# A two-layer trunk at its layer boundary: the branch output is turned to tokens in place of the sum, four chunks of weights are split ahead instead of three, and x is read a second time

## The chip, the cores and the metric

The kernel runs on one core of one Trainium2 chip. The metric is the device time of one execution in microseconds. Engines are named as in the profile: PE is TensorE (PEld its weight loads), ACT is ScalarE, DVE is VectorE, POOL is GpSimd, SP is SyncE, which issues nearly all loads.

## The reference

Two layers, each `h <- h + RMSNorm(mixer(RMSNorm(h)))`. The first mixer is differential attention, the second a pooling mixer; the boundary between them is the subject here.

```python
h = concatenate([meta, x], axis=1)                  # 272 tokens x 2048
y = diff_attention_mixer(rms_norm(h, pre_norm_g[0]), ...)   # ends in (o * silu(g)) @ w_out
h = h + rms_norm(y, post_norm_g[0])
proj = rms_norm(h, pre_norm_g[1]) @ w_in            # pooling mixer
u, g = split(proj, 2)                               # each 2048 wide
mixed = einsum(pooled(u) - u, w_group) * scale      # 4 groups, windows 2, 4, 8, 16
y = (mixed * silu(g)) @ w_out
h = h + rms_norm(y, post_norm_g[1])
return h[:, 16:]                                    # without the meta tokens
```

## The kernel before

Activations lie with features on the 128 partitions and tokens (272) along the free axis, 16 k-tiles deep. All products are in float32 made of reduced-precision parts: a chunk of weights (128x2048, 1 MB) is loaded as `raw`, cast by ACT into `hi`, and the rest `lo = raw - hi` is taken by DVE (`split`, lines 97 and 98). `mm3` makes three matmuls of each k-tile: `hi` by `hi`, `hi` by `lo`, `lo` by `hi` (lines 121 to 123). Chunks are numbered in the order of use: 64 to 79 are the output weights of attention (products `py0` to `py15`, one per chunk, 48 matmuls each), 80 to 95 the first products of the pooling mixer, `pu0` on, with the group weights of the mixing (`pm`) in between. `take` splits the chunk in use and the next and loads the one after. `raw` has two buffers, `hi` and `lo` three each, so a split waits until PE has done with the chunk three before it. Eight banks of PSUM go round in turn.

Each engine runs its instructions in one fixed order, which the framework's scheduler makes from the program text; `issue_after` pins an instruction behind another.

At the boundary (from line 541): each `py` is squared by ACT and summed by DVE into `sqy`, the last into `sqz`; ACT copies it into `yg` with the gain of the post-norm. `Norm` makes the means of squares by one-column matmuls for three groups of tokens (16, 128, 128), DVE scales them (`v`), POOL raises to -1/2, and `spread` lays the result along the free axis by three matmuls. Around that, 14 `busy` matmuls of 128 columns write a bank that nobody reads. Then for each k-tile, in nine steps of one or two k-tiles, DVE makes `yg *= pr` and `h1 += yg`, ACT the `hi` part (`hh`) with the gain of the pre-norm, DVE the `lo` part (`hl`), and PE runs the k-tile for `NS = 3` chunks at once:

```python
        for j in range(k, k + n):
            for u in range(NS):
                u_part(u, j)
```

The fourth, `pu3`, follows in quarters, with its chunk split in quarters in between (`hi_u`, `lo_u`). Chunks 84 and 85 are split into `ms`, in the home of the finished attention output. The squares of `h1` are folded by DVE into `sq1`, from which a second norm's scale is made in the middle of `pu5`. After `pu5`, `pu7`, `pu9` and `pu10`, `turn_h` turns eight blocks of `h1` to tokens (PE transposes into PSUM, ACT copies into `ht`): at the end of the program the output by tokens is `ht` plus the second branch. From `pu5` on DVE pools (`pooled`), up to the inputs `zs` of the mixing.

Of the kernel before, what the change touches and what calls it, by code (L numbers as in the profile page):

```python
# [16 lines left out]
P = 128  # L17
D = 2048
# [25 lines left out]
def trunk(ctx: ExitStack, tc: tile.TileContext, first, hT, small, gpost1, rope, w_in, w_out, p_in, p_grp, p_out, out):  # L44
# [112 lines left out]
    class Norm:  # L157
# [3 lines left out]
        def __init__(self, sq, name, r=None, more=None):  # L161
            self.pb = bank(f"rms_{name}")
            v = self.mean(sq, name, EPS)
            if more is not None:
                v = self.mean(more, name + "b", v)
            self.r = r if r is not None else const.tile([P, 3], F32, tag="nr", name=f"r_{name}")
            pool.tensor_tensor(out=self.r, in0=v, in1=mhalf, op=ALU.pow)

        def mean(self, sq, name, plus):
            c = 505 if isinstance(plus, float) else 508  # L170
# [393 lines left out]

# [268 lines left out]
```

## Time and profile before

| | |
|---|---|
| median of 3 runs | 845.69 us (845.52 to 846.54) |
| the profiled execution's own time | 845.79 us |
| its span, first to last instruction | 844.0 us |
| PE, DVE, ACT busy | 832.3, 580.0, 432.0 us |

The profile is of one execution. A matmul's row is longer than the step from one matmul to the next, since they overlap; steps are read from the starts. Matmuls of plain float32 (norm and dummies) have two rows each, transposes one.

### The profile page before, as it was taken

The page shows a single profiled execution, that of the slowest core. Times are in us where ns is not written, and L with a number is a line of the kernel's source. Part 1 is how long each engine was busy: PE and PEld are TensorE (multiplying, and loading weights), DVE is VectorE, ACT ScalarE, POOL GpSimd, SP SyncE. Part 2 cuts the span into 40 slices and gives each one's busy share as a digit, 9 for nine tenths or more (in the row PEclk, how much of TensorE's full clock was granted, in tenths as well). Part 3 has the DMA queues.
Part 4 walks back from the last instruction along what each step waited for, and adds up shares of the span by engine and source line. Part 5 has one row for each costly group of instructions (what it writes and reads, how often), then busy time and mean ns, then how long its engine had stood idle before and what let it go on. Part 6 is the DMA issues. An engine that isn't in the chain of part 4 may idle for free.

```text
span 844.0 us, 14596 instructions
## 1 busy us (share of the span) xinstructions
PE 832.3 (99%) x6140; PEld 803.3 (95%) x6140; DVE 580.0 (69%) x936; ACT 432.0 (51%) x673; POOL 7.3 (1%) x16
## 2 busy tenths in 40 slices
PE   9999999999999999999999999999999999999996
PEld 9999999999999999999999999999999888888896
DVE  6789767686868587887754444787877766685423
ACT  8646546464646466864434444544544445563420
POOL 0100000000000000000000000000000000000000
PEclk9999999999999999999999999999999999999999
DMA  9445344444444444354557455153565455545412
GB/s 352 168 151 204 149 157 164 162 164 151 150 150 151 153 158 163 128 199 152 195 206 279 174 188 211 59 201 141 196 254 184 167 199 200 189 161 206 194 50 100
DMA packets 22242, 147.27 MB, mean 174 GB/s; under 512 B 2592, under 2 KB 3104, under 8 KB 5664
## 3 DMA queue, kind: packets, MB, share of 16 engines
q1 hardware_dynamic: 22032, 146.30, 48.0%
q8 instruction: 48, 0.79, 0.4%
q14 instruction: 18, 0.15, 0.0%
q10 hardware_dynamic: 144, 0.04, 0.0%
HBM read 144.23 MB, written 2.10 MB: 173 GB/s over the span
## 4 chain that ended last, share of the span: by engine, by line
PE 94%; DVE 2%; issue 1%; DMA 1%; ACT 0%; POOL 0%; DVEq 0%; POOLq 0%; ACTq 0%
PE p L121 14%; PE p L122 14%; PE p L123 14%; PE pv L129 7%; PE py L122 4%; PE py L121 4%; PE py L123 4%; PE pv L130 4%; PE pz L725 3%; PE pz L724 3%; PE pz L723 3%; PE pu L122 3%; PE pu L123 3%; PE pu L121 3%; PE pm L129 2%
## 5 line engine op out<-in xcount | busy, mean ns | idle before, releaser
L98 DVE TENSOR_TENSOR lo<-raw,hi 128x2048 fp32r<-128x2048 f32 x121 | 276.9, 2288 | 141.5 <-ACT hi L97 141.2
L97 ACT CAST hi<-raw 128x2048 fp32r<-128x2048 f32 x121 | 231.2, 1910 | 193.0 <-PE p L122 96.0
L121 PE MATMUL p<-xs,hi 128*128 128x272 f32 x928 | 269.6, 290 | 0.0
L122 PE MATMUL p<-xs,hi 128*128 128x272 f32 x928 | 268.5, 289 | 0.0
L123 PE MATMUL p<-xs,lo 128*128 128x272 f32 x928 | 268.0, 289 | 0.0
L121 PEld LDWEIGHTS p<-xs,hi 128*128 128x128 f32 x928 | 174.9, 188 | 0.0
L123 PEld LDWEIGHTS p<-xs,lo 128*128 128x128 f32 x928 | 174.6, 188 | 0.0
L122 PEld LDWEIGHTS p<-xs,hi 128*128 128x128 f32 x928 | 174.5, 188 | 0.0
L129 PE MATMUL pv<-hs,hi 128*128 128x512 f32 x256 | 89.5, 393 | 0.0
L122 PE MATMUL py<-os,hi 128*128 128x272 f32 x256 | 74.3, 290 | 0.0
L123 PE MATMUL py<-os,lo 128*128 128x272 f32 x256 | 73.8, 288 | 0.0
L121 PE MATMUL py<-os,hi 128*128 128x272 f32 x256 | 73.7, 288 | 0.0
L130 PE MATMUL pv<-hs,lo 128*128 128x256 f32 x256 | 71.8, 280 | 0.0
L129 PEld LDWEIGHTS pv<-hs,hi 128*128 128x128 f32 x256 | 48.1, 188 | 10.9
L123 PE MATMUL pu<-hs,lo 128*128 128x264 f32 (+3 forms) x192 | 54.6, 285 | 0.0
L122 PE MATMUL pu<-hs,hi 128*128 128x264 f32 (+3 forms) x192 | 54.5, 285 | 0.0
L121 PE MATMUL pu<-hs,hi 128*128 128x264 f32 (+3 forms) x192 | 54.4, 287 | 0.0
L121 PEld LDWEIGHTS py<-os,hi 128*128 128x128 f32 x256 | 48.3, 189 | 0.0
L123 PEld LDWEIGHTS py<-os,lo 128*128 128x128 f32 x256 | 48.2, 188 | 0.0
L130 PEld LDWEIGHTS pv<-hs,lo 128*128 128x128 f32 x256 | 48.1, 188 | 0.0
L122 PEld LDWEIGHTS py<-os,hi 128*128 128x128 f32 x256 | 48.0, 188 | 0.0
L724 PE MATMUL pz<-lo,zs 128*128 128x512 f32 (+1 forms) x128 | 46.4, 363 | 0.0
(249 smaller groups left out, 1362.5 us busy)
## 6 DMA issues: line engine op xcount, KB each, us to landing
raw<-in_w_in SPq DMA_DIRECT2D x60, 1024.0 KB, 4.8
raw<-in_p_in SPq DMA_DIRECT2D x32, 1024.0 KB, 4.8
raw<-in_w_out SPq DMA_DIRECT2D x16, 1024.0 KB, 4.8
raw<-in_p_out SPq DMA_DIRECT2D x14, 1024.0 KB, 4.8
pk<-in_first SPq DMA_DIRECT2D x6, 784.0 KB, 10.7
raw<-in_p_grp SPq DMA_DIRECT2D x4, 1024.0 KB, 4.8
h<-in_hT SPq DMA_DIRECT2D x4, 544.0 KB, 7.2
rawx<-in_p_out SPq DMA_DIRECT2D x2, 1024.0 KB, 7.1
```

Source lines behind the costliest of these rows:

```text
L97: act.copy(hi[:, s], raw[i][:, s])
L98: rest[i] = dve.tensor_tensor(out=lw[:, s], in0=raw[i][:, s], in1=hi.bitcast(F32)[:, s], op=ALU.subtract)
L121: pe.matmul(o, wh, xh, start=first, stop=False)
L122: pe.matmul(o, wh, xl, start=False, stop=False)
L123: pe.matmul(o, wl, xh, start=False, stop=last)
L129: pe.matmul(ps[:, 0:2 * n], wh, x, start=first, stop=False, skip_group_check=not first)
L130: pe.matmul(ps[:, 0:n], wl, x[:, 0], start=False, stop=last)
L723: pe.matmul(ps, zh[:, k, s], wh[:, c], start=k == 0, stop=False)
L724: pe.matmul(ps, zh[:, k, s], wl[:, c], start=False, stop=False)
L725: pe.matmul(ps, zl[:, k, s], wh[:, c], start=False, stop=k == KT - 1)
```

## The change

The 32 transposes of `h1` and the 14 dummies go. In their place `yg`, the branch output with its gain but before its norm, is turned around the norm: sixteen blocks ahead of the spread, sixteen behind it. The first four banks are copied by ACT and DVE, the others by ACT between its first `hh`. Later in layer 1 DVE makes `ht = ht * rcol + xtok`, `rcol` the norm's scale by tokens and `xtok` the input x, loaded a second time by tokens into the home of `h1`. The first means (of `sqy`) move into `py15`, ahead of its last two k-tiles. Four chunks are split ahead while `py` runs: 80 and 81 into `ms`, now in the home of the attention input, from a `raw` buffer of their own (`rawu`); 82 and 83 into `hi` and `lo`. `NS` is 4, and every k-tile is a step of its own; only the first reads the spread from PSUM, the others its copy `prs`. Chunk 84 is split in two halves behind k-tile 9, chunk 85 as any other.

```diff
+            self.name, self.v = name, None
+            self.mean(sq)
+            if not wait:
+                self.power(r)
+
+        def mean(self, sq):
+        def power(self, r=None):
+            self.r = r if r is not None else const.tile([P, 3], F32, tag="nr", name=f"r_{self.name}")
+            pool.tensor_tensor(out=self.r, in0=self.v, in1=mhalf, op=ALU.pow)
...
-    def proj(ps, n0, n1, rh, rl, mid=None):
+    def proj(ps, n0, n1, rh, rl, mid=None, at=KT // 2):
...
-    NS = 3
+    NS = 4
     IU = cur[0] + KT
+
+    ms = base.tile([P, 2, 2, CW], F32R, tag="xs", name="ms")
+    ht = l1.tile([P, 2, D], F32, tag="ht", name="ht")
+    rcol = const.tile([P, 3], F32, name="rcol")
+    norm = []
-        proj(ps, 0, L, oh, ol)
-        t = sqy if m == 0 else sqz if m == KT - 1 else l1.tile([P, L], F32, tag="tmp", name=f"sqy{m}", bufs=2)
+        proj(ps, 0, L, oh, ol, (lambda: norm.append(Norm(sqy, "post0", wait=True))) if m == KT - 1 else None, KT - 3)
+        if m == KT - 1:
+            split(IU + 3)
+            break
+        t = sqy if m == 0 else l1.tile([P, L], F32, tag="tmp", name=f"sqy{m}", bufs=2)
-        if 0 < m < KT - 1:
+        if m:
...
-        if m >= KT - 5:
-
-            if m == KT - 5:
-                ht = l1.tile([P, 2, CW], F32R, tag="ht", name="w_spare")
-                split(IU, dst=(ht[:, 0, :], ht[:, 1, :]))
-            elif m >= KT - 3:
-                split(IU + m - KT + 3)
-                load(IU + m - KT + 4)
-                load(IU + m - KT + 5)
-
-
-    hs = base.tile([P, 2, KT, L], F32R, tag="xs", name="hs")
+        if m in (5, 8, 11):
+
+            q = (5, 8, 11).index(m)
+            raw[IU + q] = l1.tile([P, CW], F32, tag="rawu", name=f"rawu{q}")
+            nc.sync.dma_start(raw[IU + q], chunks[IU + q])
+        elif m == 13:
+            load(IU + 3)
+        elif m == 14:
+            split(IU + 2)
+        elif m in (7, 10):
+            q = (7, 10).index(m)
+            split(IU + q, dst=(ms[:, 0, q, :], ms[:, 1, q, :]))
+
+
+    norm = norm[0]
+    tb = [bank(f"yt{i}") for i in range(4)]
+
+    def turn_y(g, j0=0, j1=4):
+        q, b = divmod(g, 2)
+        for j in range(j0, j1):
+            i = pe.transpose(tb[g % 4][:, j * P:(j + 1) * P], yg[:, 4 * q + j, TOK[b + 1][0]:TOK[b + 1][1]], ident)
+        if j1 == 4 and g < 4:
+            turned(g, dve.tensor_copy if g in (1, 2) else act.copy)
+        return i
+
+    def turned(g, copy):
+        q, b = divmod(g, 2)
+        copy(ht[:, b, 4 * q * P:(4 * q + 4) * P], tb[g % 4])
+
+    act.square(sqz, ps[:, 0:L])
+    turn_y(0)
+    t = turn_y(1, 0, 2)
+    with tc.issue_after(t.ins):
+        norm.mean(sqz)
+    t = act.activation(yg[:, m, :], ps[:, 0:L], AF.Copy, scale=sp[:, C_POST0 + m:C_POST0 + m + 1])
+    norm.power(rcol)
+    with tc.issue_after(norm.last.ins):
+        turn_y(1, 2, 4)
+        turn_y(2)
+        t = turn_y(3)
+    with tc.issue_after(t.ins):
+        pr = norm.spread()
+        t = norm.last
+    with tc.issue_after(t.ins):
+        for g in range(4, 8):
+            t = turn_y(g)
+
...
+    prs = l1.tile([P, L], F32, name="prs")
...
-    load(i0 + NS + 1)
-    norm = Norm(sqy, "post0", more=sqz)
-    with tc.issue_after(norm.last.ins):
-        busy(5)
-    pr = norm.spread()
-    busy(9)
-    accu = [bank(f"pu{t}") for t in range(NS + 1)]
...
-    halves[i0 + NS] = (wpool.tile([P, CW], F32R, tag="hi", name="hi_u"), wpool.tile([P, CW], F32R, tag="lo", name="lo_u"))
-    k, hhs = 0, []
-    for n in (1, 1, 2, 2, 2, 2, 2, 2, 2):
-
-        ks = slice(k, k + n)
-        dve.tensor_tensor(out=yg[:, ks, :], in0=yg[:, ks, :], in1=pr.unsqueeze(1).broadcast_to([P, n, L]), op=ALU.mult)
-        dve.tensor_tensor(out=h1[:, ks, :], in0=h1[:, ks, :], in1=yg[:, ks, :], op=ALU.add)
-        for j in range(k, k + n):
-            g = sp[:, C_PRE1 + j:C_PRE1 + j + 1]
-            t = act.activation(hh[:, j, :], h1[:, j, :], AF.Copy, scale=g)
-            hhs.append(t)
-            dve.scalar_tensor_tensor(out=hl[:, j, :], in0=h1[:, j, :], scalar=g, in1=hh.bitcast(F32)[:, j, :],
+    hhs, add = [], None
+    for k in range(KT):
+
+        with (tc.issue_after(add.ins) if add else ExitStack()):
+            dve.tensor_tensor(out=yg[:, k, :], in0=yg[:, k, :], in1=prs if k else pr, op=ALU.mult)
+            if k == 0:
+                act.copy(prs, pr)
+            add = dve.tensor_tensor(out=h1[:, k, :], in0=h1[:, k, :], in1=yg[:, k, :], op=ALU.add)
+        g = sp[:, C_PRE1 + k:C_PRE1 + k + 1]
+        with (tc.issue_after(hhs[-1].ins) if hhs else ExitStack()):
+            hhs.append(act.activation(hh[:, k, :], h1[:, k, :], AF.Copy, scale=g))
+        t = dve.scalar_tensor_tensor(out=hl[:, k, :], in0=h1[:, k, :], scalar=g, in1=hh.bitcast(F32)[:, k, :],
-        for j in range(k, k + n):
-            for u in range(NS):
-                u_part(u, j)
-        k += n
-        if k in (4, 6, 8, 10):
-            with tc.issue_after(t.ins):
-                split_part(i0 + NS, slice((k - 4) * 256, (k - 2) * 256))
-        if k in (6, 8, 12, 16):
-            q = (6, 8, 12, 16).index(k)
-            for j in range(4 * q, 4 * q + 4):
-                u_part(NS, j)
-    cur[0] += 1
-
-    ms = base.tile([P, 2, 2, CW], F32R, tag="os", name="ms")
-    mh, ml = ms[:, 0], ms[:, 1]
-    with tc.issue_after(hhs[9].ins):
-        split(cur[0], dst=(mh[:, 0, :], ml[:, 0, :]))
-    load(cur[0] + 1)
+        if k < 4:
+            with tc.issue_after(hhs[-1].ins):
+                turned(4 + k, act.copy)
+        for u in range(NS):
+            u_part(u, k)
+        if k == 9:
+            with tc.issue_after(hhs[-1].ins), tc.issue_after(t.ins):
+                split(cur[0], 2)
...
-        act.square(yf[:, s], hf[:, s])
+        with tc.issue_after(hhs[min(4 * q + 7, KT - 1)].ins):
+            act.square(yf[:, s], hf[:, s])
+    load(cur[0] + 1)
-    split(cur[0] + 1, dst=(mh[:, 1, :], ml[:, 1, :]))
-
-
-    ht = l1.tile([P, 2, D], F32, tag="ht", name="ht")
...
-            if t > NS:
+            if t >= NS:
                 accu.append(bank(f"pu{t}"))
-                proj(accu[t], un0(t), L, hh, hl, (lambda: norm1.append(Norm(sq1, "pre1"))) if t == NS + 2 else None)
-                if t == NS + 2:
+                proj(accu[t], un0(t), L, hh, hl, (lambda: norm1.append(Norm(sq1, "pre1"))) if t == NS + 1 else None)
+                if t == NS + 1:
                     act.copy(r1, norm1[0].spread())
                     for i in range(t):
                         pooled(i, accu[i])
-                if t >= NS + 2:
+                if t >= NS + 1:
                     pooled(t, accu[t])
-            if t in (5, 7, 9, 10):
-                turn_h((5, 7, 9, 10).index(t))
+            if t == 7:
+                xtok = l1.tile([P, 2, D], F32, tag="h1", name="xtok")
+                for b in range(2):
+                    nc.sync.dma_start(xtok[:, b, :], xt[b * P:(b + 1) * P, :])
+            if t in (12, 13):
+
+                b = t - 12
+                with tc.issue_after(rest[cur[0]].ins):
+                    for c in (slice(0, D // 2), slice(D // 2, D)):
+                        dve.scalar_tensor_tensor(out=ht[:, b, c], in0=ht[:, b, c], scalar=rcol[:, b + 1:b + 2],
+                                                 in1=xtok[:, b, c], op0=ALU.mult, op1=ALU.add)
         elif kind == "m":
             mixing(t)
         else:
@@ -744,7 +777,7 @@
                                      op0=ALU.mult, op1=ALU.add)
             nc.sync.dma_start(out[b * P:(b + 1) * P, c], ht[:, b, c])
 
```

PE at the boundary before, from the last k-tile of `py15` to the first of `pu` (`rms_post0` is the norm's bank, `Activation`, `DVE` and `Pool` name engines waited for):

```order
L121 MATMUL py15_5998<-os_536,hi79_5936 128x272
L122 MATMUL py15_5998<-os_536,hi79_5936 128x272
L123 MATMUL py15_5998<-os_536,lo79_5937 128x272
L172 MATMUL rms_post0_6057<-ones_75,sqy_5106 128x1 [waits DVE_49]
L172 MATMUL rms_post0_6057<-ones_75,sqy_5106 128x1 x2
L172 MATMUL rms_post0_6057<-ones_75,sqz_5107 128x1 [waits DVE_49,Activation_49]
L172 MATMUL rms_post0_6057<-ones_75,sqz_5107 128x1 x2
L136 MATMUL busy_6070<-ones_75 128x128 x5
L182 MATMUL rms_post0_6057<-ident_70,r_post0_6068 128x16 [waits Pool_49]
L182 MATMUL rms_post0_6057<-ident_70,r_post0_6068 128x128 x2
L136 MATMUL busy_6079<-ones_75 128x128 x9
L121 MATMUL pu0_6089<-hs_6055,w_spare_5808 128x258 [waits PE_49,Activation_49]
```

PE at the same place now, from the last k-tile of `py15`:

```order
L121 MATMUL py15_6002<-os_536,hi79_5942 128x272
L122 MATMUL py15_6002<-os_536,hi79_5942 128x272
L123 MATMUL py15_6002<-os_536,lo79_5943 128x272
L581 MATMUL yt0_6061<-ident_70,yg_5095 128x128 x4
L581 MATMUL yt1_6062<-ident_70,yg_5095 128x128 x2
L171 MATMUL rms_post0_6045<-ones_75,sqz_5107 128x1 [waits DVE_49,Activation_49]
L171 MATMUL rms_post0_6045<-ones_75,sqz_5107 128x1 x2
L581 MATMUL yt1_6062<-ident_70,yg_5095 128x128 x2
L581 MATMUL yt2_6063<-ident_70,yg_5095 128x128 x4
L581 MATMUL yt3_6064<-ident_70,yg_5095 128x128 x4
L185 MATMUL rms_post0_6045<-ident_70,rcol_5110 128x16 [waits Pool_49]
L185 MATMUL rms_post0_6045<-ident_70,rcol_5110 128x128 x2
```

The dummies are gone, ten blocks stand between the second means and the spread and sixteen behind it, each group of four of these behind the copy of its bank; the first means stand two k-tiles ahead of the rows shown.

DVE from the second `v` on, before:

```order
L177 SCALAR_TENSOR_TENSOR v_post0b_6066<-rms_post0_6057,v_post0_6061 128x3 [waits DVE_49,PE_49]
L589 TENSOR_TENSOR yg_5095<-yg_5095,rms_post0_6057 128x272 [waits PE_49]
L589 TENSOR_TENSOR yg_5095<-yg_5095,rms_post0_6057 128x272
L590 TENSOR_TENSOR h1_5099<-h1_5099,yg_5095 128x272 [waits DVE_49] x2
L589 TENSOR_TENSOR yg_5095<-yg_5095,rms_post0_6057 128x544
L595 SCALAR_TENSOR_TENSOR hs_6055<-h1_5099,sp_67,hs_6055 128x272 [waits Activation_49] x2
L590 TENSOR_TENSOR h1_5099<-h1_5099,yg_5095 128x544 [waits DVE_49]
L589 TENSOR_TENSOR yg_5095<-yg_5095,rms_post0_6057 128x544
```

DVE from the second `v` on, now:

```order
L176 SCALAR_TENSOR_TENSOR v_post0_508_6076<-rms_post0_6045,v_post0_505_6049 128x3 [waits DVE_49,PE_49]
L588 COPY ht_5109<-yt1_6062 128x512 [waits PE_49]
L588 COPY ht_5109<-yt2_6063 128x512 [waits PE_49]
L631 TENSOR_TENSOR yg_5095<-yg_5095,rms_post0_6045 128x272 [waits PE_49]
L634 TENSOR_TENSOR h1_5099<-h1_5099,yg_5095 128x272 [waits DVE_49]
L631 TENSOR_TENSOR yg_5095<-yg_5095,prs_6114 128x272 [waits Activation_49]
L634 TENSOR_TENSOR h1_5099<-h1_5099,yg_5095 128x272 [waits DVE_49]
L638 SCALAR_TENSOR_TENSOR hs_6112<-h1_5099,sp_67,hs_6112 128x272 [waits Activation_49]
L631 TENSOR_TENSOR yg_5095<-yg_5095,prs_6114 128x272
L638 SCALAR_TENSOR_TENSOR hs_6112<-h1_5099,sp_67,hs_6112 128x272 [waits Activation_49]
```

Two copies of turned blocks stand ahead of the first product; products and sums are of one k-tile each, in turn.

DVE at the end of the k-tiles, before:

```order
L98 TENSOR_TENSOR ms_6345<-raw84_6053,ms_6345 128x2048 [waits DMAHW2_49]
L98 TENSOR_TENSOR ms_6345<-raw85_6348,ms_6345 128x2048 [waits DMAHW3_49,Activation_49]
L595 SCALAR_TENSOR_TENSOR hs_6055<-h1_5099,sp_67,hs_6055 128x272 [waits Activation_49] x2
L107 TENSOR_TENSOR yg_5095<-yg_5095 128x2176 [waits Activation_49]
L107 TENSOR_TENSOR yg_5095<-yg_5095 128x1088 [waits DVE_49]
L107 TENSOR_TENSOR yg_5095<-yg_5095 128x544 [waits DVE_49]
L98 TENSOR_TENSOR lo86_6417<-raw86_6365,hi86_6416 128x2048 [waits DMAHW4_49,PE_49,Activation_49]
```

DVE at the end of the k-tiles, now:

```order
L634 TENSOR_TENSOR h1_5099<-h1_5099,yg_5095 128x272 [waits DVE_49]
L638 SCALAR_TENSOR_TENSOR hs_6112<-h1_5099,sp_67,hs_6112 128x272 [waits Activation_49] x2
L107 TENSOR_TENSOR yg_5095<-yg_5095 128x2176 [waits Activation_49]
L107 TENSOR_TENSOR yg_5095<-yg_5095 128x1088 [waits DVE_49]
L107 TENSOR_TENSOR yg_5095<-yg_5095 128x544 [waits DVE_49]
L98 TENSOR_TENSOR lo85_6403<-raw85_6393,hi85_6402 128x2048 [waits DMAHW3_49,PE_49,Activation_49]
L107 TENSOR_TENSOR sq1_6388<-yg_5095 128x272 [waits DVE_49]
L98 TENSOR_TENSOR lo86_6458<-raw86_6406,hi86_6457 128x2048 [waits DMAHW4_49,PE_49,Activation_49]
```

Before, both splits into `ms` stood ahead of the last `hl` and of the three folds; now the split of chunk 85, `pu5`'s, stands behind the folds.

## Rows read from the trace of the kernel before

**Rows 1.** The page: the chain that ended last, share of the span by engine.
```profile
PE 94%; DVE 2%; issue 1%; DMA 1%; ACT 0%; POOL 0%; DVEq 0%; POOLq 0%; ACTq 0%
```

**Rows 2.** Chain of waits, 528 to 560 us: start, length, what.
```profile
528.92 0.40 ACT sqz L546
...
532.75 0.79 DVE yg L589 x2
...
536.33 0.63 DVE yg L589
...
539.71 0.82 DVE hs L595 x2
540.54 0.60 DVE lo_u L213
...
546.61 6.69 DMA raw<-in_p_in
...
555.25 2.29 DVE ms L98
```

**Rows 3.** Timeline of PE, 528 to 575 us: start, length, engine, line, operation.
```profile
528.59 0.29 PE L123 MATMUL py<-os,lo 128*128 128x272 f32 x1
...
529.79 0.80 PE L172 MATMUL rms_post<-ones,sqz 128*128 128x1 f32 x6 [0.34 <-ACT yg L549]
...
531.78 0.93 PE L182 MATMUL rms_post<-ident,r_post 128*128 128x16 f32 x6
...
534.50 0.38 PE L121 MATMUL pu<-hs,w_spare 128*128 128x258 f32 x1
...
554.37 0.28 PE L123 MATMUL pu<-hs,lo 128*128 128x258 f32 x1
555.70 0.39 PE L121 MATMUL pu<-hs,w_spare 128*128 128x258 f32 x1 [1.05 <-ACT hs L593]
...
560.51 0.28 PE L121 MATMUL pu<-hs,ms 128*128 128x260 f32 x1
...
568.63 0.28 PE L123 MATMUL pu<-hs,ms 128*128 128x260 f32 x1
...
569.33 0.36 PE L121 MATMUL pu<-hs,ms 128*128 128x260 f32 x1
...
571.92 0.83 PE L182 MATMUL rms_pre<-ident,r_pre 128*128 128x16 f32 x6
572.59 1.29 PE L631 MATMUL ht<-ident,h 128*128 128x128 f32 x8
573.86 0.39 PE L121 MATMUL pu<-hs,hi 128*128 128x260 f32 x1
```

**Rows 4.** Busy time by stretch, matmuls of `pu` alone: stretch, length, PE, PEld.
```profile
534.50:573.86 39.36, 35.76 (x288) 34.74 (x288) 0.00 (x0) 1.00 0.37 134
```

**Rows 5.** Timeline of PE at a later block of transposes; the tile `ht`.
```profile
585.30 0.28 PE L123 MATMUL pu<-hs,lo 128*128 128x260 f32 x1
...
586.22 0.37 PE L121 MATMUL pu<-hs,hi 128*128 128x264 f32 x1
...
L632 ACT COPY ht<-ht x8: 570/585/597, 573.2 to 612.7; 128x512 f32<-128x512 f32 x8
```

**Rows 6.** Timeline of DVE, 500 to 580 us.
```profile
526.89 0.43 DVE L548 TENSOR_TENSOR sqy<-sqy,sqy 128x272 f32<-128x272 f32 x1
...
558.29 4.50 DVE L107 TENSOR_TENSOR yg<-yg 128x2176 f32<-128x2176 f32 x3
```

**Rows 7.** The tile `py` (first and last start); loads by line, us to landing.
```profile
L121 PE MATMUL py<-os,hi x256: 287/288/289, 431.9 to 528.3; 128*128 128x272 f32 x128
...
gp<-in_gpost SPq DMA_DIRECT2D x1, 1024.0 KB, 10.2
```

**Rows 8.** Timeline of PE at the start of the program.
```profile
6.72 0.42 PE L237 MATMUL pq<-xs,flo 128*128 128x272 f32 x1
6.95 0.32 PE L238 MATMUL pq<-xs,fhi 128*128 128x272 f32 x1
```

More of the change, by code (lines that the diff above doesn't have):

```diff
@@ L43, in trunk @@
 @with_exitstack
-def trunk(ctx: ExitStack, tc: tile.TileContext, first, hT, small, gpost1, rope, w_in, w_out, p_in, p_grp, p_out, out):
+def trunk(ctx: ExitStack, tc: tile.TileContext, first, hT, xt, small, gpost1, rope, w_in, w_out, p_in, p_grp, p_out, out):
     nc = tc.nc
@@ L157, in trunk, with __init__ @@
     class Norm:
-        def __init__(self, sq, name, r=None, more=None):
+        def __init__(self, sq, name, r=None, wait=False):
             self.pb = bank(f"rms_{name}")
[L163 to L170, printed above, removed]
+            self.name, self.v = name, None
[3 more added lines that the diff above has]
+        def mean(self, sq):
+            c = 505 if self.v is None else 508
             for j in range(3):
                 self.last = pe.matmul(self.pb[:, c + j:c + j + 1], sq[:, WIN[j]:WIN[j] + P], ones[:, 0:1], start=True, stop=True)
-            v = const.tile([P, 3], F32, tag="nv", name=f"v_{name}", bufs=2)
-            if isinstance(plus, float):
-                self.vi = dve.tensor_scalar(out=v, in0=self.pb[:, c:c + 3], scalar1=1.0 / D, scalar2=plus, op0=ALU.mult, op1=ALU.add)
-            else:
-                dve.scalar_tensor_tensor(out=v, in0=self.pb[:, c:c + 3], scalar=1.0 / D, in1=plus, op0=ALU.mult, op1=ALU.add)
-            return v
+            v = const.tile([P, 3], F32, tag="nv", name=f"v_{self.name}_{c}", bufs=2)
+            if self.v is None:
+                self.vi = dve.tensor_scalar(out=v, in0=self.pb[:, c:c + 3], scalar1=1.0 / D, scalar2=EPS, op0=ALU.mult, op1=ALU.add)
+            else:
+                dve.scalar_tensor_tensor(out=v, in0=self.pb[:, c:c + 3], scalar=1.0 / D, in1=self.v, op0=ALU.mult, op1=ALU.add)
+            self.v = v
+        def power(self, r=None):
+            self.r = r if r is not None else const.tile([P, 3], F32, tag="nr", name=f"r_{self.name}")
+            pool.tensor_tensor(out=self.r, in0=self.v, in1=mhalf, op=ALU.pow)
         def spread(self):
             for j, (a, b) in enumerate(TOK):
-                pe.matmul(self.pb[:, a:b], self.r[:, j:j + 1].broadcast_to([P, P]), ident[:, 0:b - a], start=True, stop=True)
+                self.last = pe.matmul(self.pb[:, a:b], self.r[:, j:j + 1].broadcast_to([P, P]), ident[:, 0:b - a], start=True, stop=True)
             return self.pb[:, 0:L]
@@ L289, in proj @@
                 rh[:, k, n0:n1], rl[:, k, n0:n1], k == 0, k == KT - 1)
-            if mid and k == KT // 2:
+            if mid and k == at:
                 mid()
@@ L562, in trunk @@
+    hs = base.tile([P, 2, KT, L], F32R, tag="os", name="hs")
     hh, hl = hs[:, 0], hs[:, 1]
     r1 = l1.tile([P, L], F32, name="r1")
+    prs = l1.tile([P, L], F32, name="prs")
     def un0(t):
@@ L570, in trunk @@
     load(i0 + NS)
-    load(i0 + NS + 1)
-    norm = Norm(sqy, "post0", more=sqz)
-    with tc.issue_after(norm.last.ins):
-        busy(5)
-    pr = norm.spread()
-    busy(9)
-    accu = [bank(f"pu{t}") for t in range(NS + 1)]
+    accu = [bank(f"pu{t}") for t in range(NS)]
     def u_part(t, k):
@@ L618, in trunk @@
         s = slice(4 * q * L, 4 * (q + 1) * L)
-        act.square(yf[:, s], hf[:, s])
+        with tc.issue_after(hhs[min(4 * q + 7, KT - 1)].ins):
+            act.square(yf[:, s], hf[:, s])
+    load(cur[0] + 1)
     with tc.issue_after(rest[cur[0]].ins):
         fold(yg, sq1)
-    split(cur[0] + 1, dst=(mh[:, 1, :], ml[:, 1, :]))
-    ht = l1.tile([P, 2, D], F32, tag="ht", name="ht")
-    def turn_h(q):
-        for b in range(2):
-            ps = bank(f"ht{q}_{b}")
-            for j in range(4):
-                pe.transpose(ps[:, j * P:(j + 1) * P], h1[:, 4 * q + j, TOK[b + 1][0]:TOK[b + 1][1]], ident)
-            act.copy(ht[:, b, 4 * q * P:(4 * q + 4) * P], ps)
     mx = base.tile([P, KT, SEQ], F32, tag="big", name="mx")
-    zs = base.tile([P, 2, KT, SEQ], F32R, tag="os", name="zs")
+    zs = base.tile([P, 2, KT, SEQ], F32R, tag="xs", name="zs")
     zh, zl = zs[:, 0], zs[:, 1]
@@ L745, in out_store @@
             nc.sync.dma_start(out[b * P:(b + 1) * P, c], ht[:, b, c])
-    es = base.tile([P, 2, 2, CW], F32R, tag="xs", name="es")
+    es = base.tile([P, 2, 2, CW], F32R, tag="os", name="es")
     eh, el = es[:, 0], es[:, 1]
@@ L811 @@
         "hT": hT,
+        "xt": np.ascontiguousarray(A(x)[0]),
         "small": np.ascontiguousarray(np.concatenate([
```

## The prediction

> **What bounds the kernel now.** The page comes first: PE holds 94% of the chain that ended last [rows 1]. So the time is PE's work plus the places where PE stands or does work that serves nothing, and a change pays only by making those smaller. The chain of waits in order of time shows one such place: from 528.9 to 558 us, the boundary between the layers, the chain leaves PE, first for the norm, then for VectorE's 272- and 544-wide steps, then for a load of `raw` and the split of `ms` behind it [rows 2]. PE's own timeline says what that stretch costs [rows 3]. The last product matmul of `py15` starts at 528.59 and the first of `pu` at 534.50: 5.91 us, filled with norm matmuls and the 14 `busy` dummies. From there to the first matmul of `pu6` at 573.86 lie 39.36 us with 288 `pu` matmuls in them [rows 4]. Their step is (568.63 - 560.51) / 68 = 0.1194 us, over 69 matmuls in a row, so the 288 need 34.39 us. Around them stand three means of the second norm (568.63 to 569.33 less one step: 0.58), its spread (571.92 to 572.59: 0.67) and eight transposes with a wait (572.59 to 573.86: 1.27). What remains, 39.36 - 34.39 - 0.58 - 0.67 - 1.27 = 2.45 us, are stalls of PE in the first four `pu`; the largest, 554.37 to 555.70 less a step, is 1.21. Three more blocks of eight transposes follow later; one of them, 585.30 to 586.22 less one step, holds PE's path for 0.80 us [rows 5].
>
> **The change, part by part.** *Turning moves.* The 32 transposes of `h1` leave the path of the products: 1.27 + 3 x 0.80 = 3.67 us. The 32 of `yg` that take their place stand where the dummies stood. A block of eight takes 0.80, so one costs 0.10.
>
> *Does the boundary hold them?* The three means of `sqy` go into `py15`, six matmuls before its end, at about 528.0. `sqy` is then ready: its last add ended at 526.89 + 0.43 = 527.32 [rows 6], and the split ahead of it starts with `py15` now as before. The means cost 0.58, so `py15`'s last matmul starts at 529.17. ScalarE's square started 0.33 behind that matmul and took 0.40 [rows 2, 3]: 529.50 to 529.90. PE turns six blocks meanwhile, to 529.9, and starts the second means at 530.0. That is 0.21 later than the 529.79 of before, when the first means, which came just ahead, kept them waiting. From there the links keep their distances [rows 2, 3]: the spread 1.99 behind the second means, at 532.0, and VectorE's first product 2.96 behind them, at 532.96. The means hold PE until about 530.75, then ten transposes (1.0) fit ahead of the spread. The spread holds PE 0.67 like the second norm's, and the last sixteen transposes end at 534.3. They need the banks of the first sixteen emptied, two copies on each of two engines. ScalarE's copy of 128x512 takes 0.585 [rows 5]; VectorE's is not in the trace, and I bound it by that 0.585 from below and by 0.63 from above, the step of its 544-wide product that reads PSUM [rows 2]; I take 0.63. With ScalarE at 530.3 and 532.1 and VectorE at 531.2 and 531.85, all are empty by 532.7, ahead of the sixteen and of the first product.
>
> *First `pu`.* Before, it came 1.75 behind VectorE's first product, with a second product ahead of the first sum; now the sum comes first, up to 0.36 sooner. That gives 534.35 to 534.71 by the chain and 534.3 by PE's queue; I take 534.62, 0.12 later than before. The next kind of matmul needs `hl` of k-tile 0, now behind product 1, which waits for the copy `prs`, and sum 1: a stall of 0 to 0.4 behind four matmuls, taken as 0.34.
>
> *Four chunks instead of three.* From there PE needs 12 x 0.1194 = 1.43 us per k-tile. VectorE needs a product, a sum and an `hl`: two products or two `hl` take 0.79 and 0.82, so 0.36 to 0.41 each, 1.18 in all with some dependence. Before, it was the reverse: per two k-tiles 0.63 + 0.63 + 0.82, mostly with 0.60 for a quarter of `lo_u` [rows 2], 1.34 per k-tile, against PE's 9 x 0.1194 = 1.07. So PE becomes the bound of this stretch, and its stalls shrink from 2.45 to 0.34. The load at 546.61 leaves the chain as well: `raw84` gets a buffer that is free once `py15`'s own chunk is split.
>
> *The rest at nothing.* Four extra splits instead of three lie beside `py`; a product lasts (528.3 - 431.9) / 16 = 6.0 us [rows 7], and two splits take VectorE 4.58 [rows 2] and ScalarE less. If they were not covered, a split would cost up to 2.29. `xtok`'s two loads go out behind the squares, about 556, ahead of `raw87`; with the 10.2 us of the longest 1 MB load there [rows 7] they land by 566, `pu7` is due at 576. The scaled add of the residual is four operations of 1024 elements in the middle of layer 1, at two steps of 0.63 each 5.0 us; they have the next chunk's time to hide in, and uncovered they would cost that.
>
> **Sum** against the profiled 845.79 us: - 3.67 (transposes) - 2.45 + 0.34 (stalls) + 0.12 (start) = - 5.66. The median is 0.10 lower, so 840.1 us by the median. Late next is the split of chunk 85 for `pu5`, since it stands behind the folds: VectorE ends its k-tiles at about 554.8 (532.96 + 16 x 1.18, 2.4 for chunk 84, 0.5 waiting for ScalarE), the last squares end at some 556.3, the folds take 4.4 to 4.5 [rows 6], the split 2.29: 563.0 to 563.1. PE is there at 534.62 + 0.34 + 240 x 0.1194 = 563.6, and needs `lo` two steps on: 0.7 in hand.
>
> **The rivals.** *The clock falls.* From 529.3 to 534.6 PE would have 32 transposes and nine small norm matmuls, and no dummies. At the start of the program rows show the lower level: 272-wide matmuls step by 0.23 us up to 6.95 us [rows 8], the 1.2 GHz level, 0.22 for 258 columns, against 0.1194 at the boundary. If transposes do not keep the clock up, `pu` starts on that level; if it lasts as long as at the start, some 6 us, it costs 6 x (1 - 0.1194 / 0.22) = 2.7 us, and sixteen slow transposes up to 1.6 more: 842.8, at worst 844.4. For it: every dummy goes. Against it: spread and eight transposes, 1.94 us from 571.92 on, left the clock as it was, and PE's rows at 573.86 and later step as before [rows 3]; but that is a third of the length. The Trainium skill ("TensorE: Matmul & The Clock Gate", Part 4: PE-mode transpose) says that transposes do not count as PE activity in the way other matmuls do and that the full clock does not engage for them. By that rule it would be 842.8; no run here shows a stretch of transposes this long.
>
> *PE waits for VectorE further on.* Chunk 85 has 0.7 us in hand, and the pooling that follows does not come earlier as PE does. A split late by its own length costs 2.29 - 0.7 = 1.6 us, with 1 to 2.5 as the bounds: 841.1 to 842.6.
>
> *The boundary does not hold the transposes.* If the copies are late and the last sixteen stand idle, their 1.6 us come back, and if VectorE's steps then take as long as before, the 2.1 us of stalls: 843.8, and 844 to 845.5 with a late copy or two on top: no change.
>
> *Slower.* ScalarE's queue has the cast of the first early chunk ahead of a square of `py` and of the cast of chunk 71, and its load goes out at about 448 into the traffic of `h1` and the gains. Chunk 71 is due with `py7`, 431.9 + 7 x 6.0 = 474, and some 9 us of casts and splits lie ahead of it. A load that lands by 465 costs nothing, each us later one; from 25 us in flight the loss passes 5.7 + 1.7 and the kernel is slower. The longest load there took 10.2 [rows 7].
>
> **How the numbers follow.** Forecast as summed, 839.0 to 841.1: 0.62. Clock: 0.18. VectorE late: 0.11. Not held: 0.05. Slower: 0.04. The range for 8 in 10 takes the forecast, the VectorE case and most of the clock case: 838.9 to 843.0. A measurement of this kernel tells about 0.2%, 1.7 us, from no change. The clock and VectorE cases still end below 844.0, so faster 0.91, same 0.05, slower 0.04.
>
> **What would show it.** Right: some 5.4 us from `py15`'s last matmul to `pu`'s first with all 32 transposes in it, none after; from there to `pu6` 36.0 us instead of 39.4; one short stall behind the first four `pu` matmuls; the chain on PE through the four `pu`. Wrong: `pu` steps of over 0.2 us behind the boundary (clock); PE idle before `pu5` or the first mixing, ended by VectorE; transposes behind the spread that wait for copies.

## The result and the profile after

The changed kernel takes 840.89 us (median of 4 runs, 839.84 to 842.11) against 846.12 for the kernel before; the ratio is 0.9936, 95% interval 0.992 to 0.9952. That is 5.2 us less, where 5.6 were forecast (840.1, range 838.9 to 843.0). The profiled execution took 839.84 us, its span 838.1. The chain that ended last lies on PE for 96% now, against 94% before [rows 1].

```profile
PE 96%; issue 1%; DMA 1%; POOL 0%; DVE 0%; ACT 0%; SPq 0%; DVEq 0%; POOLq 0%; ACTq 0%
```

PE's timeline of the changed kernel over the boundary (start, length, engine, line, operation; `yt` are the banks of the turned blocks), to be read beside that of before [rows 3]:

```profile
529.20 0.29 PE L123 MATMUL py<-os,lo 128*128 128x272 f32 x1
529.33 0.81 PE L581 MATMUL yt<-ident,yg 128*128 128x128 f32 x6
529.99 0.83 PE L171 MATMUL rms_post<-ones,sqz 128*128 128x1 f32 x6
530.67 1.29 PE L581 MATMUL yt<-ident,yg 128*128 128x128 f32 x10
532.00 0.94 PE L185 MATMUL rms_post<-ident,rcol 128*128 128x16 f32 x6
532.77 1.91 PE L581 MATMUL yt<-ident,yg 128*128 128x128 f32 x16
534.50 0.51 PE L121 MATMUL pu<-hs,ms 128*128 128x258 f32 x2
...
535.25 0.39 PE L122 MATMUL pu<-hs,ms 128*128 128x258 f32 x1
...
569.96 0.83 PE L185 MATMUL rms_pre<-ident,r_pre 128*128 128x16 f32 x6
...
570.54 0.36 PE L121 MATMUL pu<-hs,hi 128*128 128x260 f32 x1
```

`py15`'s last matmul starts at 529.20, `pu`'s first at 534.50: 5.30 us with all 32 transposes in them, and no idle time of PE that ends in a wait for another engine. The one stall is the expected one: four matmuls of `pu` from 534.50 on would end their steps at 534.98, the fifth starts at 535.25, 0.27 later. `pu6` starts at 570.54, 36.04 us behind the first `pu`; before it was 39.36 [rows 3, 4].

VectorE's timeline at the same place:

```profile
531.12 1.29 DVE L588 COPY ht<-yt 128x512 f32<-128x512 f32 x2
532.97 0.44 DVE L631 TENSOR_TENSOR yg<-yg,rms_post 128x272 f32<-128x272 f32 x1 [0.56 <-PE rms_post L185]
533.44 0.44 DVE L634 TENSOR_TENSOR h<-h,yg 128x272 f32<-128x272 f32 x1
...
534.70 0.49 DVE L638 SCALAR_TENSOR_TENSOR hs<-h,sp,hs 128x272 fp32r<-128x272 f32 x1
...
556.14 4.51 DVE L107 TENSOR_TENSOR yg<-yg 128x2176 f32<-128x2176 f32 x3 [1.50 <-ACT yg L653]
560.57 2.28 DVE L98 TENSOR_TENSOR lo<-raw,hi 128x2048 fp32r<-128x2048 f32 x1
```

The two copies take 0.645 each (forecast 0.63), the first product starts at 532.97 (forecast 532.96), the folds at 556.14 instead of 558.29 [rows 6], the split of chunk 85 ends at 562.85 (forecast 563.0). The first product waits for the spread, not for the copies.

In the profiles of this study the first matmul of `py`, ahead of which nothing was changed, starts anywhere from 431.4 to 434.3 us, and the times of one kernel scatter by 2 us or more. So the experiments below are read by stages counted from that matmul, and by medians only beside it. The stages are differences of starts in PE's timeline, in us: from `py`'s first matmul to `pu`'s first, from there to `pu6`'s first, from there to the first of the last product (`pz`).

| kernel | py to pu | pu to pu6 | pu6 to pz | py to pz | median, us |
|---|---|---|---|---|---|
| before | 102.63 | 39.36 | 173.51 | 315.50 | 845.2 to 845.9 |
| changed | 102.69 | 36.04 | 170.80 | 309.53 | 840.89 |
| changed, again | 102.68 | 36.05 | 170.79 | 309.52 | 840.25 |
| turn_back_dummies | 104.28 | 37.24 | 173.44 | 314.96 | 844.56 |
| turn_back_bare | 103.39 | 39.66 | 173.45 | 316.50 | 846.37 |
| before_no_turn | 102.63 | 38.09 | 170.79 | 311.51 | 842.79 |
| quarters | 102.68 | 36.57 | 170.79 | 310.04 | 840.74 |
| late85 | 102.69 | 208.15 to pz | | 310.84 | 841.29 |
| long_turns | 116.59 | 35.73 | 170.79 | 323.11 | 854.75 |
| no_xtok | 102.69 | 36.04 | 170.79 | 309.52 | 840.19 |
| half_turn | 102.67 | 37.44 | 170.79 | 310.90 | 841.44 |
| before_bare | 103.34 | 40.11 | 173.49 | 316.94 | 846.51 |

(In late85 the second norm's spread stands inside `pu6`, so its last two stages are one. The medians of before are of three groups of runs, each beside the experiments of its group; beside the result it was 846.12.) In py to pz the change is worth 309.53 - 315.50 = -5.97 us: +0.06 to the first `pu`, -3.32 to `pu6`, -2.71 behind it. Forecast were +0.12, -3.38 (1.27 and 2.45 less 0.34) and -2.40.

### The profile page after: what moved, and what is told of

Same layout as the page of the kernel before. It is cut to its first block, busy times and chain, and to the rows that moved or that the text cites. A ratio compares the mean times of both kernels' runs of the same rounds, so it can differ in the third digit from the quotient of the medians.

```text
span 838.1 us, 14551 instructions
## 1 busy us (share of the span) xinstructions
PE 826.7 (99%) x6112; PEld 798.7 (95%) x6112; DVE 585.3 (70%) x954; ACT 431.4 (51%) x670; POOL 7.3 (1%) x16
## 4 chain that ended last, share of the span: by engine, by line
PE 96%; issue 1%; DMA 1%; POOL 0%; DVE 0%; ACT 0%; SPq 0%; DVEq 0%; POOLq 0%; ACTq 0%
PE p L121 14%; PE p L123 14%; PE p L122 14%; PE pv L129 7%; PE py L121 4%; PE py L123 4%; PE py L122 4%; PE pu L122 4%; PE pu L121 4%; PE pu L123 4%; PE pv L130 4%; PE pz L758 3%; PE pz L756 3%; PE pz L757 3%; PE pm L129 2%
## 5 line engine op out<-in xcount | busy, mean ns | idle before, releaser
L98 DVE TENSOR_TENSOR lo<-raw,hi 128x2048 fp32r<-128x2048 f32 (+1 forms) x123 | 279.1, 2270 | 137.3 <-ACT hi L97 137.1
L97 ACT CAST hi<-raw 128x2048 fp32r<-128x2048 f32 (+1 forms) x123 | 233.0, 1896 | 190.9 <-PE p L122 96.0
L123 PE MATMUL pu<-hs,lo 128*128 128x260 f32 (+3 forms) x224 | 63.7, 285 | 0.0
L121 PE MATMUL pu<-hs,hi 128*128 128x260 f32 (+3 forms) x224 | 63.7, 285 | 0.0
L122 PE MATMUL pu<-hs,hi 128*128 128x260 f32 (+3 forms) x224 | 63.6, 284 | 0.0
```

Source lines behind the costliest of these rows:

```text
L97: act.copy(hi[:, s], raw[i][:, s])
L98: rest[i] = dve.tensor_tensor(out=lw[:, s], in0=raw[i][:, s], in1=hi.bitcast(F32)[:, s], op=ALU.subtract)
L121: pe.matmul(o, wh, xh, start=first, stop=False)
L122: pe.matmul(o, wh, xl, start=False, stop=False)
L123: pe.matmul(o, wl, xh, start=False, stop=last)
```

## The experiments

**The changed kernel again**, to stand beside the others of its group.

> The changed kernel as it is, beside the three others of this group, to size their differences. Theory (the sum of the prediction): 840 to 841 us; last matmul of py15 to first of pu 5.3 us, from there to the first of pu6 36.1 to 36.2 us, granted clock 1.00 in both stretches. Rival (the clock falls behind the boundary in some executions, since no busy dummies are left): the runs scatter by more than those of before, with a lower mean clock in the longer ones, and a profile that falls on such a run shows pu steps of over 0.2 us behind the boundary.

Measured: 840.25 us (839.21 to 841.22, 5 runs), ratio to before 0.9941 (0.9925 to 0.9957); stages equal to the first profile within 0.01 us, granted clock 1.00 over the boundary. The runs of before in this group scatter no less (843.71 to 847.79, but for one of 2097.43) than the five. The clock rival finds nothing here.

**The turning put back, with the dummies.**

```diff
-    turn_y(0)
-    t = turn_y(1, 0, 2)
-    with tc.issue_after(t.ins):
-        norm.mean(sqz)
+    norm.mean(sqz)
...
-        turn_y(1, 2, 4)
-        turn_y(2)
-        t = turn_y(3)
...
-        for g in range(4, 8):
-            t = turn_y(g)
...
+    with tc.issue_after(norm.last.ins):
+        busy(5)
+    pr = norm.spread()
+    busy(9)
...
-                        dve.scalar_tensor_tensor(out=ht[:, b, c], in0=ht[:, b, c], scalar=rcol[:, b + 1:b + 2],
-                                                 in1=xtok[:, b, c], op0=ALU.mult, op1=ALU.add)
+            if t in (5, 7, 9, 10):
+                turn_h((5, 7, 9, 10).index(t))
```

> The changed kernel with the turning put back to where it was (h1 after pu5, pu7, pu9 and pu10), with the 14 dummies at the boundary and no second read of x. Theory: the boundary keeps its 5.3 us, since the norm's chain sets it with the transposes or without; the four blocks cost 1.27 + 3 x 0.80 = 3.67 us again: 840.9 + 3.7 = 844.5 us. Rival (the transposes fill the boundary to the brim and set its length): the boundary is shorter by 0.3 us or more, and the kernel ends at 844.2 us or below. Rival (the second read of x and its scaled add cost something): below 844 us too, but with the boundary at 5.3.

Measured: 844.56 us (843.96 to 845.99, 11 runs), ratio to before 0.9992 (0.9983 to 1.0002). The blocks cost 37.24 - 36.04 = 1.20 ahead of `pu6` and 173.44 - 170.80 = 2.64 behind it, 3.84 together. But the boundary did not keep its length in this profile: 104.28 instead of 102.69, and the reason is the granted clock. Busy time by stretch: stretch, length, PE's busy time and matmuls, granted clock, DMA share and GB/s:

```profile
530.00:532.00 2.00, 1.63 (x13) 0.92 0.78 324
532.00:534.00 2.00, 2.00 (x11) 0.50 0.00 0
534.00:536.00 2.00, 2.00 (x15) 0.73 0.00 0
536.00:538.00 2.00, 2.00 (x19) 1.00 0.00 0
```

It fell to 0.50, the 1.2 GHz level, from just before 532 to about 535, with six small norm matmuls (three means and the spread) and 14 dummies as PE's work behind `py15`; spread and dummies then ran at half speed, and `pu` waited for the last of them. The time came out as the theory has it (844.5), but in part by luck: the theory had the boundary at 5.3 us and this profile has 6.89. The stages of this profile add up to 5.43 us more than the changed kernel's, the medians to 4.3; the profiled execution, 845.55 us, is the second longest of the eleven.

**The same without dummies** (the diff above without the `busy` lines).

> As turn_back_dummies, without the 14 dummies: PE has nothing but nine small norm matmuls for 5.3 us. If it is PE's work in the boundary (dummies or transposes) that keeps the clock up, pu starts at steps of 0.22 us as at the program's start, and some 6 us of that cost 2.7: 847.2 us, granted clock well under 1.00 behind 534 us. If a gap of this length does not matter to the clock: 844.5 us as with the dummies, granted clock 1.00, and neither the dummies nor the transposes were needed for it.

Measured: 846.37 us (845.07 to 847.64, 12 runs), ratio 1.0008 (0.9997 to 1.0019): the gain of the four chunks is gone. The windows and PE's timeline behind the boundary show why:

```profile
530.00:532.00 2.00, 1.04 (x8) 0.95 0.92 389
532.00:534.00 2.00, 1.28 (x6) 0.50 0.00 0
534.00:536.00 2.00, 0.44 (x3) 0.50 0.00 0
536.00:538.00 2.00, 2.00 (x9) 0.50 0.03 8
538.00:540.00 2.00, 2.00 (x12) 0.50 0.00 0
540.00:542.00 2.00, 2.00 (x11) 0.50 0.00 0
542.00:544.00 2.00, 2.00 (x18) 0.99 0.00 0
```

```profile
537.17 0.42 PE L123 MATMUL pu<-hs,ms 128*128 128x258 f32 x1
537.38 0.42 PE L122 MATMUL pu<-hs,ms 128*128 128x258 f32 x1
```

The step of `pu` is 0.21 from 535.93 to 542. Against turn_back_dummies the stage from `pu` to `pu6` is 39.66 - 37.24 = 2.42 longer; forecast for this case were 2.7. The slow spread makes the boundary longer too, by 103.39 - 102.69 = 0.70 against the changed kernel, which the forecast left out. So with next to no work for PE in the boundary the clock fell, and whatever takes the dummies' place has to be looked at for it.

**The kernel before without its transposes**, and without the copies behind them.

```diff
-            if t in (5, 7, 9, 10):
-                turn_h((5, 7, 9, 10).index(t))
...
-                scalar=r, in1=ht[:, b, c],
+                scalar=r, in1=gp1[:, c],
```

> The kernel before with its 32 transposes of h1 and their copies left out; the output then leaves out h1 (the norm's gain is added in its place, at the same cost). It takes the first term of the sum alone. Theory: 3.67 us less than before, 846.1 - 3.7 = 842.4 us, and pu's first matmul at 5.9 us behind py15 and pu6 1.27 us sooner. Rival (the blocks of transposes gave VectorE's pooling time that PE then waits for): one or two us less gained, 843.5 to 844.5 us, with PE idle ended by DVE before the mixing.

Measured: 842.79 us (842.38 to 843.84, 9 runs), ratio 0.9971 (0.9961 to 0.9981), so 2.5 us less, with 1.6 to 3.3 as bounds. The stages say more: 38.09 against 39.36 ahead of `pu6`, 1.27 as read; 170.79 against 173.51 behind it, 2.72 instead of 2.40. Together 3.99, 0.32 above the term. Of the gap between 3.99 and the whole-run difference this profile shows 0.7 at the end of the program (97.36 us from `pz` to the end of the span, 96.63 before, and from `pz` to VectorE's last operations 90.34 against 90.33, so it lies in the store); the rest stays open.

Most of the 0.32 lies in the first matmul behind a block: 3 x 0.08 = 0.24. The kernel before, at the block that the prediction read [rows 5]:

```profile
585.42 1.03 PE L631 MATMUL ht<-ident,h 128*128 128x128 f32 x8
...
586.42 0.28 PE L122 MATMUL pu<-hs,hi 128*128 128x264 f32 x1
```

The block's start to the `pu` matmul at 586.22 is the 0.80 that was counted; that matmul's own step to 586.42 is 0.20 instead of 0.12, and so belongs to the block as well: 0.88 of the 0.91 that each of the three later blocks gave back.

**Three chunks in the steps, the fourth in quarters**, with the new splits and homes.

```diff
-        for u in range(NS):
+        for u in range(NS - 1):
             u_part(u, k)
+        if k in (5, 7, 11, 15):
+            q = (5, 7, 11, 15).index(k)
+            for j in range(4 * q, 4 * q + 4):
+                u_part(NS - 1, j)
```

> The changed kernel with three chunks in the k-tile steps and the fourth, pu3, in quarters behind k-tiles 5, 7, 11 and 15, as the kernel before has it; splits, homes and VectorE's steps stay those of the changed kernel. Theory of the prediction (four chunks make PE the bound, 1.43 us per k-tile against VectorE's 1.18 to 1.34): PE is the faster again with 1.07, and the stalls of the kernel before come back, about 2.1 us: 842.4 us. Rival (what stalled PE was VectorE's other work in that stretch, two splits of 2.29 and four quarters of 0.60 and a load, of which 2.35 are left): with VectorE's rows of the changed kernel, PE's waits add up to 1.0 instead of 0.2, most of it behind the split of chunk 84: 841.1 us.

Measured: 840.74 us (839.65 to 841.64, 6 runs), ratio 0.9942 (0.9928 to 0.9957); `pu` to `pu6` 36.57, 0.53 more than the changed kernel. The theory's 2.1 did not come back. Of the 2.05 us that this stretch gained beyond its block of transposes (38.09 to 36.04), 0.53 hang on running four chunks in step. The other 1.5 belong to what this kernel shares with the changed one: VectorE has one split in that stretch (chunk 84 in two halves, 2.35 us together) where it had two into `ms`, one of them behind the load of `raw`, and the quarters [rows 2], and it goes by single k-tiles.

The trace of the kernel before says which of these weighs most. VectorE and ScalarE there, ahead of PE's longest stall, the one that ends at 555.70 with a wait for ScalarE's `hs` [rows 3]:

```profile
550.85 0.72 DVE L590 TENSOR_TENSOR h<-h,yg 128x544 f32<-128x544 f32 x1
...
553.32 1.90 ACT L97 CAST ms<-raw 128x2048 fp32r<-128x2048 f32 x1 [2.92 <-DMA raw<-in_p_in]
...
555.13 0.93 ACT L593 ACTIVATE hs<-h,sp 128x272 fp32r<-128x272 f32 x2
```

The last `h1` was summed at 551.57, but ScalarE's queue had the cast of chunk 85 ahead of the last two `hs`: it stood idle for 2.92 us until that chunk's load had landed, then cast for 1.90. PE lost 1.21 by it, and another 0.30 at 557.60, where VectorE's last `hl` came behind the second split [rows 2]; 1.51 in all. Behind neither place does PE wait in the changed kernel or in this one, where the cast of chunk 85 comes after the last `hs`. No run moves that cast alone.

**The split of chunk 85 made late.**

```diff
+        with tc.issue_after(t.ins):
+            t = dve.tensor_tensor(out=yg[:, 8:16, :], in0=yg[:, 8:16, :], in1=h1[:, 8:16, :], op=ALU.add)
+        dve.tensor_tensor(out=sq1.unsqueeze(1), in0=yg[:, 0:1, :], in1=yg[:, 1:2, :], op=ALU.add)
+    with tc.issue_after(t.ins):
+        split(cur[0] + 1)
```

> The changed kernel with one more VectorE operation of 2176 elements (about 2.4 us) between the folds and the split of chunk 85, and the last fold (0.35) ahead of that split; its result is not used. It tests the 0.7 us that the prediction gave this split in hand; the profile after has lo85 end at 562.85 and pu5's third matmul start at 563.67, 0.8. Theory: lo85 ends 2.75 later, PE waits 2.75 - 0.8 = 1.95 us ahead of pu5's third matmul and nowhere else: 842.2 us. Rival (later waits of PE on pooling hide it or add to it): under 841.2 us, or over 843 with PE idle ended by DVE before the first mixing.

Measured: 841.29 us (840.48 to 842.41, 6 runs); from `pu` to `pz` 208.15 instead of 206.84, so 1.31 for a split that starts 2.71 later, counted from `pu` (forecast 2.75). VectorE and PE of this kernel:

```profile
560.39 2.42 DVE L661 TENSOR_TENSOR yg<-yg,h 128x2176 f32<-128x2176 f32 x1
...
563.08 4.49 DVE L98 TENSOR_TENSOR lo<-raw,hi 128x2048 fp32r<-128x2048 f32 x2
```

```profile
563.58 0.72 PE L171 MATMUL rms_pre<-ones,sq 128*128 128x1 f32 x6
564.16 0.37 PE L121 MATMUL pu<-hs,hi 128*128 128x260 f32 x1
...
565.42 0.39 PE L123 MATMUL pu<-hs,lo 128*128 128x260 f32 x1 [0.77 <-DVE lo L98]
...
600.48 0.28 PE L122 MATMUL pu<-hs,hi 128*128 128x264 f32 x1
600.78 0.39 PE L123 MATMUL pu<-hs,lo 128*128 128x264 f32 x1
```

The wait for `lo85` is there. What this split had in hand was 0.95 rather than the 0.8 counted: in the changed kernel it ends at 562.85, and `pu5`'s third matmul starts at 563.80. The price is lower than the 1.95 expected, because the scheduler put the means of the second norm, 0.58 that PE has to do anyway, in front of the waiting matmul; PE idled for 0.77 there and lost 1.0 by the starts. The other 0.28 come at 600.48 to 601.00, where PE waits for a later `lo` that ends at 600.72; the theory had no second wait.

**A long stretch of transposes**, 128 more behind the spread.

```diff
         for g in range(4, 8):
+            for _ in range(8):
+                for j in range(4):
+                    pe.transpose(tb[g % 4][:, j * P:(j + 1) * P], yg[:, 4 * (g // 2) + j, TOK[g % 2 + 1][0]:TOK[g % 2 + 1][1]], ident)
             t = turn_y(g)
```

> The changed kernel with 128 more transposes of yg into the same banks behind the spread, each block of four eight times more: PE does nothing but transposes for some 14.5 us. If transposes keep the clock up: a step of 0.10 us throughout, granted clock 1.00, pu starts 12.8 us later and, since VectorE is far ahead by then, runs without its stall: 840.5 + 12.8 - 0.3 = 853 us. If they do not count as work of PE: the granted clock falls to 0.50 within the stretch, the steps double, pu starts at 0.22 us a step, and the kernel takes 860 us or more.

Measured: 854.75 us (853.63 and 855.88), `pu`'s first matmul 13.9 us later than in the changed kernel: (15.64 - 1.73) / 128 = 0.109 us a transpose. The window over all 144:

```profile
535.22:550.86 15.64, 15.64 (x146) 1.00 0.00 1
550.86:560.00 9.14, 9.14 (x79) 1.00 0.33 115
```

The clock stays at 1.00 through 15.6 us of nothing but transposes and in `pu` behind them. The stall behind the first four matmuls is gone as expected (35.73 against 36.04).

**Without the second read of x** and its scaled add.

```diff
-                    nc.sync.dma_start(xtok[:, b, :], xt[b * P:(b + 1) * P, :])
...
-                        dve.scalar_tensor_tensor(out=ht[:, b, c], in0=ht[:, b, c], scalar=rcol[:, b + 1:b + 2],
-                                                 in1=xtok[:, b, c], op0=ALU.mult, op1=ALU.add)
```

> The changed kernel without the second read of x and without the four operations that scale ht and add it; the output then leaves out the scaled residual. Theory (hidden): the same as the changed kernel within 0.3 us, 840.2 to 840.9. Rival (the 5.0 us of VectorE or the 2 MB of loads cost something): faster by up to 1 us or more, and PE's time from pu6 to pz shorter than 170.8 us.

Measured: 840.19 us (839.48 to 841.72, 6 runs), stages equal to the changed kernel's within 0.01. The four operations take 1.27 each, 5.1 us in all (forecast 5.0), and nothing waits for them:

```profile
L724 DVE SCALAR_TENSOR_TENSOR ht<-ht,rcol,xtok x4: 1268/1271/1272, 617.1 to 623.6; 128x1024 f32<-128x1024 f32 x4
```

**Half the transposes**, none behind the spread.

```diff
-        for g in range(4, 8):
-            t = turn_y(g)
+        pass
```

> The changed kernel without the sixteen transposes behind the spread (the copies stay and move old contents of the banks, so half of the turned residual is not that of the reference). Theory (the norm's chain sets the first pu, PE's queue of transposes is only just shorter): from py15's last matmul to pu's first 5.2 to 5.3 us as with all 32, time 840 to 841 us, as long as the clock stays at 1.00. Rival (PE's queue sets it): 0.3 us or more sooner. For the clock: PE has nothing between the spread and pu, about 1.8 us; if sixteen transposes ahead of it are enough the granted clock stays 1.00, if not it falls behind 532 us and pu starts at 0.22 us a step, 1 to 2.5 us longer.

Measured: 841.44 us (839.67 to 843.37, 9 runs). `py` to `pu` is 102.67, as with 32: the norm's chain sets the start of `pu`, and PE's queue of transposes fits under it. The clock fell, later than in the bare boundary:

```profile
534.00:536.00 2.00, 0.44 (x4) 1.00 0.00 0
536.00:538.00 2.00, 2.00 (x11) 0.54 0.00 0
538.00:540.00 2.00, 2.00 (x13) 0.61 0.00 0
540.00:542.00 2.00, 2.00 (x19) 1.00 0.00 0
```

PE's timeline has nothing between the spread and `pu`, 1.56 us idle by the row:

```profile
533.18 0.93 PE L185 MATMUL rms_post<-ident,rcol 128*128 128x16 f32 x6
535.67 0.51 PE L121 MATMUL pu<-hs,ms 128*128 128x258 f32 x2 [1.56 <-ACT hs L636]
```

The fall cost 37.44 - 36.04 = 1.40 us in this execution; the medians lie 0.6 to 1.2 apart. The sixteen behind the spread are no burden to the path, and without them the clock fell. Whether it is their number or their place that held it was not taken apart.

**The kernel before without its dummies** (the two `busy` lines out).

> The kernel before without its 14 dummies, nothing else changed: what they were worth there, and so what the change could lose by dropping them. If work on PE in the boundary holds the clock (as the bare boundary of the changed kernel suggests): the granted clock falls to 0.50 behind 532 us for some 10 us, and the kernel takes 1.5 to 2.5 us longer than before, 847.3 to 848.3 us (part of it hidden, since VectorE sets the pace behind the boundary there). If the dummies did nothing: 845.6 us, clock 1.00.

Measured: 846.51 us (845.91 to 848.08, 10 runs), ratio 1.0017 (1.0007 to 1.0027), 1.4 us more; the stages give 0.71 + 0.75 = 1.46 up to `pu6`. The clock is at 0.50 from about 531 to 541. The first row is of the kernel before, the others of this one:

```profile
532.00:534.00 2.00, 2.00 (x19) 1.00 0.00 0
...
530.00:532.00 2.00, 0.81 (x4) 0.70 0.31 131
532.00:534.00 2.00, 0.95 (x4) 0.50 0.03 8
...
540.00:542.00 2.00, 2.00 (x15) 0.74 0.00 0
```

## Why the prediction was right, and where not

**Turning moves: right, mis-sized.** The term of 3.67 measured 3.99 (before_no_turn, stages): 1.27 for the first block, as read, and 0.91 instead of 0.80 for each of the others. The price of a block was read up to the start of the next matmul, and not to the end of that matmul's longer step.

**The boundary holds them: right.** The spread starts at 532.00 (forecast 532.0), the last sixteen transposes begin at 532.77 and fit, the first `pu` starts 0.06 later in its stage (forecast 0.12). half_turn shows that it would not start sooner with sixteen fewer. (The prediction counts nine norm matmuls between `py15` and `pu`; there are six, since the first three means stand inside `py15`.) The case in which they stand idle for the copies did not occur.

**Stalls: the size right, the reason given only a part of it.** Forecast 2.45 less 0.34 = 2.11, measured 2.05; the stall that remains is 0.27. The prediction put it as "So PE becomes the bound of this stretch", because four chunks give PE 1.43 us per k-tile. With three chunks in step and the fourth in quarters PE has 1.07 per k-tile again, and only 0.53 comes back. The larger part, 1.51 by the rows of before, is the stall behind the cast and split of chunk 85 and the load that they waited for. The prediction has that load in a side sentence, as chunk 84's, though the cast of 84 ran at 545.51, ahead of it; it hung the gain on the count of chunks. That the size came out is luck to this extent.

**The clock: the rival did not occur, and its rule is wrong here.** The change took all dummies away, and both profiles of it show 1.00 over the boundary, as do the four of other kernels with all 32 transposes there (quarters, late85, long_turns, no_xtok). That the price was real is seen without the transposes: 0.50 behind 532, `pu` at 0.21 a step, 2.4 us from `pu` on and 0.7 ahead of it. The transposes hold the clock: 32 did over 5.3 us, 144 over 15.6. The Trainium skill ("TensorE: Matmul & The Clock Gate", Part 4: PE-mode transpose) says the opposite, that transposes do not count as PE activity like other matmuls and that the full clock does not engage for them. In these runs the measurement decides against it, for transposes of plain float32 that come when the clock is already up; no run here shows transposes raising it.

**VectorE late: not reached.** Chunk 85 had 0.95 in hand (forecast 0.7), and late85 shows that delay beyond it does cost time: 1.31 for 2.71 - 0.95 = 1.76.

**The early loads: right.** The slower case asked for 25 us in flight; `rawu`'s three loads landed in 5.2 to 9.0:

```profile
DMA to landing us min/median/max: 5.2/7.0/9.0
```

**The sum.** -5.66 forecast against -5.97 between `py` and `pz`: the transposes gave 0.32 more, the stalls 0.06 less, the start 0.06 more. The medians give 5.2 and 5.3, with intervals from 3.6 to 6.8 us, since the scatter lies ahead of `py`.

## What to carry to other kernels

Work that must be done on the bounding engine is free where that engine waits for a chain of others; measure the chain with less work first (here 5.3 us with 32 transposes and with 16), then fill it. If dummy work stood in the gap, look at the granted clock with the filler in its place: with sixteen transposes and 1.56 us of idle PE ahead of the product it fell and cost 1.4 us, with 32 it did not. And when a stall goes away, undo one cause at a time before naming it, and read which engine ended the wait: here the count of chunks in step was a quarter of it, and the longest stall stood behind a cast on ScalarE that waited for its load.

## What was not expected of the hardware

Fourteen dummy matmuls of 128 columns did not hold the clock in the profile of turn_back_dummies (0.50 from 532 to about 535), while the same fourteen held it in the kernel before (1.00), where three more one-column means stood beside them and no `py` matmuls came between. The mean clock of the executions of the two bare kernels is 0.991 to 0.994 in all 22, that of the changed kernel 0.995 to 0.998, so without filler the fall probably happens every time. The mean also counts the end of the program, where the clock falls with PE empty (0.50 behind 840 us in turn_back_dummies), so it can show a fall of ten us, but not one of three: turn_back_dummies has 0.995 to 0.998 in its eleven executions, and its fall need not be in each. One execution of the kernel before, 847.53 us, has 0.993. What decides between the two kernels with dummies stays open.
